# Half-height and half-width products held until their partner is ready, and the meta keys' product cut into such pairs

## The chip, the cores and the metric

The kernel runs on one core of a Trainium2 chip. The metric is the device time of one launch in microseconds, the median of several executions. TensorE (PE) multiplies, ScalarE (ACT) and VectorE (DVE) work on what it leaves in PSUM, GpSimd (POOL) does little, and SyncE (SP) issues most loads.

## What is computed

Three layers run in one launch over 512 positions of width 1024, in float32: a hybrid layer with a feed-forward part, then layer "ab" and layer "cd" over the 512 positions and 16 meta tokens ahead of them. The change touches four pieces of the last two layers:

```python
# layer ab, eight heads of 64: each query attends to its 128 best keys
logits = einsum('bqhd,bqkhd->bhqk', qb, kg) * dh ** -0.5 + bias
p = softmax(where(ok, logits, NEG_INF_2))
out = einsum('bhqk,bqkhd->bqhd', p, vg)
# layer ab, gated linear attention, and layer cd, retention: four heads of 64 (values 128)
att = where(causal, q @ k.T, 0)                  # retention: times a decay matrix
o = att @ v + (q * decay_in) @ S                 # S: state before the block
S = S * decay + (k * decay_out).T @ v
# layer cd, stick breaking: eight heads of 64
w = exp(log_sigmoid(z) + after)                  # z = q @ k.T, masked
out = einsum('bhqs,bshd->bqhd', w, v)
```

## The kernel before

Most of PE's work is the projections: `f_acc` (L164) multiplies a 128x128 block of weights with 256, 272 or 512 positions, three products for each block (high by high, high by low, low by high part in fp32r). While a projection runs, `tick` steps a generator of `self.bg` (L85), in which the attention and the linear layers stand as pipelines (`pipe`). So a few small products at a time stand between the projections' products. The order on each engine is then made by the framework's scheduler from the program's dependences and priorities (`first`, `chain`), and PE runs its list strictly in that order.

Four kinds of small product use a part of the 128x128 array. All four are plain float32, and each leaves two records in the trace:

- Values of the chosen keys (`dsa`, function `values`). For a pair of heads `f` and a block of 128 queries `i`, L1109 gives the 64 channels of head `e` = 0 in rows 0 to 63 of `o` and those of `e` = 1 in rows 64 to 127, for each block `j` of 128 keys. So a product has 128 rows of the array and 64 columns, and the two heads' use different columns. The 16 meta keys of both heads stand in one product at L1111 with 48 rows: rows 0 to 15 for one head, 32 to 47 for the other, and `avm` holds zeros elsewhere. Its right side comes from `em` (L1083), which `turn` transposes (L194) and copies out of PSUM (L1097).
- `linear`, scores (L1235) and state part (L1260): 64 channels of a head are rows 0 to 63 or 64 to 127, and heads with `e` = 0 and 1 use different rows and write different PSUM tiles. L1258 beside them uses the whole array, and L1213 (`update`) 64 columns.
- `stick`, values (L1354): 128 keys by 64 columns for each of two heads (`i` = 0, 1), for a block `b` of keys and 16 to 512 queries. Their right sides are the exponentials `wt` of L1342, one for each head.

For the two heads of one step the pipelines give the two products one after the other in the program, but nothing keeps them together in PE's order.

Of the kernel before, what the change touches and what calls it, by code (L numbers as in the profile page):

```python
# [8 lines left out]
F32 = mybir.dt.float32  # L9
# [3 lines left out]
AF = mybir.ActivationFunctionType  # L13
# [6 lines left out]
M = 16  # L20
# [40 lines left out]
class Kern:  # L61
# [56 lines left out]
    def behind(self, ins, name):  # L118

        if name and name != ins.name:  # L120
            self.tc.add_manual_dep(ins, name, mybir.DependencyInfo(mybir.DependencyClass.NoSync, mybir.DependencyReason.DATA), reason="order")

    def queue(self, q, out, src):

# [771 lines left out]
    def layer_ab(self, act, acc):  # L896
        nc, tc = self.nc, self.tc
# [3 lines left out]
        with tc.tile_pool(name="ab", bufs=1, reuse_waits="tile") as p:  # L901
# [30 lines left out]
            with self.chain():  # L932
                ps = self.ch("b")
# [61 lines left out]

            av = p.tile([128, 4, 512], F32, name="av")

            avm = p.tile([48, 4, 128], F32, name="avm")
            em = [p.tile([128, 48], F32, name=f"em{b}") for b in range(2)]
            for t in (avm, *em):  # L1000
                nc.gpsimd.memset(t, 0.0)

# [5 lines left out]
            av = av, avm, em  # L1008
# [41 lines left out]
    def dsa(self, p, cols, av, ag, masks, segs):  # L1050

        f, qs, ks = cols
        nc = self.nc
        av, avm, em = av
        bh = p.tile([128, 2, T], F32, name="bh", bufs=1)
        self.sheared(bh, self.tab2[2 * f:2 * f + 2], N2)
        tiles = {}
        held = []

        def logits(i, hh):  # L1060
# [24 lines left out]

        def turn(i, hh, n, q0, W, e, d):
            pT = p.tile([128, 5, 128], F32, name="pT", bufs=3)
            nb = i + 1
            if nb:
                pt = self.ch("b")  # L1090
                for j in range(nb):
                    self.transpose(pt[:, j * 128:(j + 1) * 128], e[:, M + j * 128:M + (j + 1) * 128])
                nc.scalar.copy(pT[:, :nb], pt[:, :nb * 128].rearrange("p (j q) -> p j q", j=nb))
            if hh == 1:
                pt = self.ch("b")
                self.transpose(pt[:48, :n], em[i % 2][:n])
                nc.vector.tensor_copy(pT[:48, 4, :n], pt[:48, :n])  # L1097
            return i, hh, n, q0, pT, d

        def values(i, hh, n, q0, pT, d):  # L1100
            held.append(pT)
            if hh == 0:
                return
            o = self.ch("o")[:, :n]

            for j in range(i + 1):
                for e in range(2):
                    c = (2 * f + e) * 64
                    nc.tensor.matmul(o[64 * e:64 * e + 64], lhsT=av[:, j, c:c + 64], rhs=held[e][:, j, :n], start=j == 0, stop=False,  # L1109
                                     skip_group_check=True)  # L1110
            nc.tensor.matmul(o, lhsT=avm[:, f], rhs=pT[:48, 4, :n], start=i < 0, stop=True, skip_group_check=True)  # L1111
            held.clear()
            rd = p.tile([128, 128], F32, name="rd", bufs=2)
            nc.vector.reciprocal(d[:n], d[:n])
            nc.scalar.copy(rd[:n].rearrange("p (h d) -> p h d", h=2), d[:n].to_broadcast([n, 2, 64]))
            return n, q0, o, rd

# [74 lines left out]
    def linear(self, p, q, k, kx, qs, ks, v, vm, decay, att, masked, out, meta, pace):  # L1192
# [3 lines left out]
        nc = self.nc  # L1196
# [28 lines left out]
        def scores(t, c0, n, vv):  # L1225
            if t == 0 and not meta:
                keys(-1, 0, M)
            if t < 3:
                keys(t, c0, n)
            a = att(t)  # L1230
            ps = self.ch("a"), self.ch("a")

            pairs = [(f, e, 64 * e) for f in range(2) for e in range(2)]
            for f, e, r0 in pairs:
                nc.tensor.matmul(ps[e][:n, f * n:f * n + n], lhsT=k[r0:r0 + 64, f, c0:c0 + n], rhs=q[r0:r0 + 64, f, c0:c0 + n], start=True, stop=True)  # L1235
            if kx is not None and n > 64:
                for f, e, r0 in pairs:
                    nc.tensor.matmul(ps[e][:64, f * n + 64:f * n + n], lhsT=kx[r0:r0 + 64, f, c0:c0 + 64], rhs=q[r0:r0 + 64, f, c0 + 64:c0 + n],
                                     start=True, stop=True)
            with self.chain():  # L1240
                for e in range(2):
                    masked(a[:n, e::2, :n], ps[e][:n, :2 * n].rearrange("p (h c) -> p h c", h=2), n, e)
            return t, c0, n, vv, a

        def attend(t, c0, n, vv, a):
            if t == 0 and not meta:
                update(-1, vm, M)
            st = state[0]
            osq = p.tile([128, T], F32, name="osq", tag="e", bufs=4 if meta else 2)[:, :512].rearrange("p (h c) -> p h c", h=4)
            rs = p.tile([128, 4], F32, name="rs", bufs=2)  # L1250
            om = self.ch("o"), self.ch("b")
            for inter in range(1 if st is None else 2):
                for f in range(2):
                    for e in range(2):
                        h, r0 = 2 * f + e, 64 * e
                        o = om[e][:n, f * 128:f * 128 + 128]
                        if not inter:
                            nc.tensor.matmul(o, lhsT=a[:n, h, :n], rhs=vv[:n, h * 128:h * 128 + 128], start=f == 0, stop=st is None, skip_group_check=True)  # L1258
                        else:
                            nc.tensor.matmul(o, lhsT=qs[r0:r0 + 64, f, c0:c0 + n], rhs=st[r0:r0 + 64, f], start=False, stop=True, skip_group_check=True)  # L1260
# [27 lines left out]
    def stick(self, p, cols, dv, od):  # L1288


        f, qs, ks = cols
        nc = self.nc
        om = []
        total = [None, None]
        held = []
# [29 lines left out]
        def sums(hh, b, n, c0, w, z, L, parts):  # L1325
# [16 lines left out]
            nc.scalar.activation(wt, z, AF.Exp)  # L1342
            return hh, b, n, c0, wt

        def values(hh, b, n, c0, wt):
            held.append(wt)
            if hh == 0:
                return
            if not om:
                om.append(self.ch("o"))  # L1350

            for i in range(2):
                h = 2 * f + i
                nc.tensor.matmul(om[0][64 * i:64 * i + 64, c0 - M:], lhsT=dv[:n, b, h * 64:h * 64 + 64], rhs=held.pop(0),  # L1354
                                 start=b == 4, stop=b == 0, skip_group_check=True)
            if b == 0:
                with self.chain():
                    nc.vector.tensor_tensor(out=od[:, f, M:], in0=om[0], in1=od[:, f, M:], op=OP.mult)
# [350 lines left out]
```

## Time and profile before

| | |
|---|---|
| Median of 3 runs | 1211.96 us (1211.02 to 1212.45) |
| The profiled execution | 1211.16 us |
| Its span, first to last instruction | 1209.4 us |
| PE busy, share of the span | 98% |
| DVE, ACT, POOL busy | 66%, 51%, 4% |
| Share of PE in the chain that ended last | 89% |
| Granted TensorE clock, mean | 0.995 |

The profiled execution took 1.8 us more than its span, and 0.8 us less than the median. Busy time of PE counts each product from its start to its modelled end, and products overlap in it, so what a product costs is read from the distance of starts.

### The profile page before, as it was taken

Reading aid. Unit: us, or ns where it says so; the run is one execution under the profiler, and the core shown is the slowest. Engines: PE = TensorE matmul, PEld = TensorE weight load, DVE = VectorE, ACT = ScalarE, POOL = GpSimd, SP = SyncE. Lnnn points to the kernel's source line nnn. Section 1 sums busy time; section 2 is a strip of 40 time slices with the busy share of each in tenths; the row PEclk is TensorE's granted clock in tenths of the full one; section 3 lists DMA queues with packets and bytes.
Section 4 is the critical chain, followed back from the end, with each engine's and each line's share of the span. In section 5 each row is a group of like instructions: output and inputs, shape, how many; then the busy total and the mean of one; then the engine's idle time right before and its main releaser. Section 6 shows DMA issues by size and latency. Waiting matters only on the chain.

```text
span 1209.4 us, 18772 instructions
## 1 busy us (share of the span) xinstructions
PE 1186.9 (98%) x7150; PEld 1014.7 (84%) x7150; DVE 800.5 (66%) x1810; ACT 618.7 (51%) x1377; POOL 51.4 (4%) x79
## 2 busy tenths in 40 slices
PE   8999899999999999999999999999999999999997
PEld 7988678888888888888999899888899889876776
DVE  6999966444434444455799999656575576775772
ACT  5588556333323333344454355666463575575753
POOL 7000002000000000011000000000020000000000
PEclk9999999999999999999999999999999999999999
DMA  7321122323233332234221122222132213220121
GB/s 253 110 78 60 46 71 88 103 89 105 72 98 113 102 97 95 85 96 123 89 71 61 46 71 71 70 71 71 54 111 84 87 53 106 70 70 18 53 87 70
DMA packets 32906, 101.81 MB, mean 84 GB/s; under 512 B 4128, under 2 KB 4960, under 8 KB 32816
## 3 DMA queue, kind: packets, MB, share of 16 engines
q1 hardware_dynamic: 30784, 96.48, 25.6%
q0 software_dynamic: 880, 2.25, 0.7%
q10 hardware_dynamic: 1152, 1.89, 0.5%
q8 instruction: 56, 0.92, 0.3%
q14 instruction: 34, 0.28, 0.1%
HBM read 96.42 MB, written 3.10 MB: 82 GB/s over the span
## 4 chain that ended last, share of the span: by engine, by line
PE 89%; DVE 6%; ACT 3%; DMA 1%; issue 1%; DVEq 0%; ACTq 0%
PE mm L164 68%; PE psb L194 4%; PE mm L183 2%; PE pso L1354 1%; DVE wlo L150 1%; PE pso L1109 1%; PE psa L1479 1%; PE mm L1479 1%; ACT whi L149 1%; PE pso L1111 1%; PE pso L642 1%; DVE sc L965 1%; PE psa L1328 1%; DMA x<-in_x 1%; PE psa L1073 1%
## 5 line engine op out<-in xcount | busy, mean ns | idle before, releaser
L164 PE MATMUL mm<-hhi,whi 128*128 128x512 f32 (+2 forms) x1280 | 433.5, 339 | 0.0
L164 PE MATMUL mm<-hlo,whi 128*128 128x512 f32 (+2 forms) x1280 | 426.6, 333 | 0.0
L164 PE MATMUL mm<-hhi,wlo 128*128 128x512 f32 (+2 forms) x1280 | 426.5, 333 | 0.0
L149 ACT CAST whi<-wraw 128x512 fp32r<-128x512 f32 x346 | 205.4, 594 | 314.2 <-PE mm L164 294.9
L150 DVE TENSOR_TENSOR wlo<-wraw,whi 128x512 fp32r<-128x512 f32 x346 | 231.5, 672 | 143.5 <-ACT whi L149 120.0
L164 PEld LDWEIGHTS mm<-hhi,whi 128*128 128x128 f32 x1280 | 242.4, 189 | 23.9 <-issue 2.0
L164 PEld LDWEIGHTS mm<-hhi,wlo 128*128 128x128 f32 x1280 | 241.9, 189 | 21.7 <-issue 0.3
L164 PEld LDWEIGHTS mm<-hlo,whi 128*128 128x128 f32 x1280 | 242.1, 189 | 21.0 <-issue 0.2
L164 PE MATMUL mm<-mx,whi 128*128 128x512 f32 (+2 forms) x448 | 112.8, 340 | 5.2 <-ACT mx L112 4.5
L164 PEld LDWEIGHTS mm<-mx,whi 128*128 128x128 f32 x448 | 76.2, 191 | 17.2 <-ACT mx L112 5.6
L786 DVE TENSOR_TENSOR gu<-mm,rb 128x512 f32<-128x512 f32 x44 | 30.4, 692 | 68.9 <-PE mm L164 66.8
L164 PE MATMUL mm<-mx,wlo 128*128 128x512 f32 (+2 forms) x224 | 74.8, 334 | 0.0
L164 PE MATMUL mm<-hidh,whi 128*128 128x512 f32 x176 | 68.5, 389 | 0.0
L164 PE MATMUL mm<-hidl,whi 128*128 128x512 f32 x176 | 68.5, 389 | 0.0
L164 PE MATMUL mm<-hidh,wlo 128*128 128x512 f32 x176 | 68.5, 389 | 0.0
L256 POOL TENSOR_TENSOR acc<-acc,sq 128x528 f32<-128x528 f32 (+1 forms) x18 | 25.7, 1428 | 778.1 <-ACT sq L254 461.0
L326 DVE TENSOR_TENSOR tmp<-mm,rb 128x272 f32<-128x272 f32 (+2 forms) x76 | 35.7, 469 | 27.4 <-PE mm L164 26.8
L164 PEld LDWEIGHTS mm<-mx,wlo 128*128 128x128 f32 x224 | 42.7, 190 | 3.5
L681 DVE SCALAR_TENSOR_TENSOR y<-u,cols,y 128x512 f32<-128x512 f32 x60 | 42.7, 745 | 1.2 <-ACT y L679 1.0
L314 DVE TENSOR_TENSOR x<-x,mm 128x512 f32<-128x512 f32 (+2 forms) x56 | 30.0, 536 | 15.5 <-PE mm L164 15.0
L164 PEld LDWEIGHTS mm<-hidh,whi 128*128 128x128 f32 x176 | 33.0, 188 | 6.9
L164 PEld LDWEIGHTS mm<-hidl,whi 128*128 128x128 f32 x176 | 33.0, 188 | 6.9
(434 smaller groups left out, 1794.9 us busy)
## 6 DMA issues: line engine op xcount, KB each, us to landing
wraw<-in_w SPq DMA_DIRECT2D x144, 512.0 KB, 3.5
wraw<-in_w SPq DMA_DIRECT2D x16, 384.0 KB, 3.0
wraw<-in_w SPq DMA_DIRECT2D x16, 320.0 KB, 2.8
bh<-tab SPq DMA_DIRECT2D x16, 132.0 KB, 2.9
mx<-cqk SPq DMA_DIRECT2D x8, 132.0 KB, 2.4
x<-in_x SPq DMA_DIRECT2D x4, 256.0 KB, 5.3
B<-tab POOLq DMA_DIRECT2D x4, 256.0 KB, 7.2
out<-L ACTq DMA_DIRECT2D x4, 256.0 KB, 2.5
```

Of the source, the lines that this page charges most:

```text
L149: self.nc.scalar.copy(hi[:, :w], raw[:, c])
L150: self.lo.tensor_tensor(out=lo[:, :w], in0=raw[:, c], in1=hi[:, :w].bitcast(F32), op=OP.subtract)
L164: nc.tensor.matmul(ps[b], lhsT=ww[i][:, f0:f0 + nf], rhs=aa[:, t0:t1], start=first and i == 0 and j == 0, stop=last and i == n - 1 and j == 2)
L183: nc.tensor.matmul(part(t), lhsT=aa[:, t0:t0 + nt], rhs=ww[i], start=u + i + j == 0 and t % 2 == 0, stop=u == 1 and i == 3 and j == 2, ski ...
L194: self.nc.tensor.transpose(out, in_, self.ident[:n, :n])
L256: e.tensor_tensor(out=acc[:, c0:c1], in0=acc[:, c0:c1], in1=sq[:, c0:c1], op=OP.add)
L314: nc.vector.tensor_tensor(out=x, in0=x, in1=p, op=OP.add)
L326: self.nc.vector.tensor_tensor(out=out[:, t0:t1], in0=p, in1=rb[:nf, t0:t1], op=OP.mult)
L642: nc.tensor.matmul(o[:, h * 64:h * 64 + 64], lhsT=pT[:, j * 128:(j + 1) * 128], rhs=vt[:, j, h * 64:h * 64 + 64], start=j == 0, stop=j == i)
L681: nc.vector.scalar_tensor_tensor(y[:, f], u[:, f, k:k + S], cw[:, f, k:k + 1], y[:, f], op0=OP.mult, op1=OP.add)
L786: nc.vector.tensor_tensor(out=t[:, g], in0=ps, in1=rbx, op=OP.mult)
L1479: nc.tensor.matmul(ps[half], lhsT=aa[:, c], rhs=ww[:, :512], start=False, stop=k == 3 and j == 2, skip_group_check=True)
```

## The change

`one_by_one` chains the products of the linear layers' scores and attention in the order of the program, in which the two halves of the array take turns. `ready` lets the first product of a pair wait for what the second needs as well: in `values` of `dsa` the first product of a block waits for the copies of head 1 (`made[1]`), in `stick` the first of two waits for the second's exponential. The meta keys' product becomes two, one for each head, with 128 rows and 64 columns, as the others of its block; for that `avm` and `em` grow to 128 rows or columns of which most are zero, and the copy at L1097 moves from DVE to ACT and from 48 rows to 128.

```diff
+    def one_by_one(self, inss):
+        for a, b in zip(inss, inss[1:]):
+            self.behind(b.ins, a.ins.name)
+
+    def ready(self, ins, names):
+        for name in names:
+            self.tc.add_manual_dep(ins, name, ...Sync...)
...
-            avm = p.tile([48, 4, 128], F32, name="avm")
-            em = [p.tile([128, 48], F32, name=f"em{b}") for b in range(2)]
+            avm = p.tile([128, 4, 128], F32, name="avm")
+            em = [p.tile([128, 128], F32, name=f"em{b}") for b in range(2)]
...
             if hh == 1:
                 pt = self.ch("b")
-                self.transpose(pt[:48, :n], em[i % 2][:n])
-                nc.vector.tensor_copy(pT[:48, 4, :n], pt[:48, :n])
+                self.transpose(pt[:, :n], em[i % 2][:n])
+                made[hh].append(nc.scalar.copy(pT[:, 4, :n], pt[:, :n]).ins.name)
...
-            for j in range(i + 1):
+            for j in [*range(i + 1), 4]:
                 for e in range(2):
                     c = (2 * f + e) * 64
-                    nc.tensor.matmul(o[64 * e:64 * e + 64], lhsT=av[:, j, c:c + 64], rhs=held[e][:, j, :n], start=j == 0, stop=False,
-                                     skip_group_check=True)
-            nc.tensor.matmul(o, lhsT=avm[:, f], rhs=pT[:48, 4, :n], start=i < 0, stop=True, skip_group_check=True)
+                    w, x = (avm[:, f, 64 * e:64 * e + 64], pT) if j == 4 else (av[:, j, c:c + 64], held[e])
+                    ins = nc.tensor.matmul(o[64 * e:64 * e + 64], lhsT=w, rhs=x[:, j, :n], start=i < 0 or j == 0, stop=j == 4,
+                                           skip_group_check=True)
+                    if j in (0, 4) and e == 0 and (i < 0 or j == 0):
+                        self.ready(ins.ins, made[1])
...
+            self.one_by_one(inss)      # linear: after the scores, and after the attention's products
...
-                nc.tensor.matmul(om[0][64 * i:64 * i + 64, c0 - M:], ...)   # stick
+                ins = nc.tensor.matmul(om[0][64 * i:64 * i + 64, c0 - M:], ...)
+                if i == 0:
+                    self.ready(ins.ins, [name])
```

The next rows are of PE's list before, second pair of heads (`f` = 1), first block of queries. L1109 is a head's product, L1111 the meta keys', L194 a transposition, L1073 to L1076 logits, L164 a projection.

```order
L1109 MATMUL pso<-pT,av 64x128
L164 MATMUL mm<-hhi,wlo 128x256
L194 MATMUL psb<-keep,em_6251 48x128
L1109 MATMUL pso<-pT,av 64x128
L1073 MATMUL psa<-qk 128x400
L1074 MATMUL psa<-qk 128x400
L1076 LDWEIGHTS identb
L1076 MATMUL psa<-mk_5945,identb 128x400
L194 MATMUL psb<-keep,e 128x128 x2
L1111 MATMUL pso<-pT,avm 128x128
```

The same block in the changed kernel, where the lines are some ten to twenty further down (L1122 for L1109 and L1111, L204 for L194, L1084 for L1073):

```order
L204 MATMUL psb<-keep,em_6251 128x128
L204 MATMUL psb<-keep,e 128x128 x2
L1084 MATMUL psa<-qk 128x272
L1085 MATMUL psa<-qk 128x272
L1122 MATMUL pso<-pT,av 64x128 x2
L1122 MATMUL pso<-pT,avm 64x128 x2
```

The two heads' products moved together and behind the transposition of `em`, and the meta keys' product became a pair right behind them.

In layer cd, third pair of heads of `stick` (L1354) beside the start of retention (L1213 state, L1235 scores), PE's list before reads:

```order
L1354 MATMUL pso<-wt,dv 64x512
L1328 MATMUL psb<-Lh,trir 128x512
L194 MATMUL psb<-keep,mx 128x128 x2
L1328 MATMUL psb<-Ll,trir 128x512
L1333 MATMUL psb<-Sh,mones 128x400
L1333 MATMUL psb<-Sl,mones 128x400
L1213 MATMUL psb<-cvm,kst 64x128 x4
L1235 MATMUL psa<-cqk 128x128
L1354 MATMUL pso<-wt,dv 64x512
```

The same two values now (L1373), with four scores (L1250) ahead of them:

```order
L1347 MATMUL psb<-Ll,trir 128x512
L1352 MATMUL psb<-Sh,mones 128x400
L1352 MATMUL psb<-Sl,mones 128x400
L1250 MATMUL psa<-cqk 128x128 x4
L1373 MATMUL pso<-wt,dv 64x512 x2
```

The first value moved behind all that stood between it and its partner.

A little later in that list, one block of retention's attention before (L1258 within the block, L1260 with the state):

```order
L1258 MATMUL psb<-cv,att 128x128 x2
L1260 MATMUL psb<-S,mx 128x128 x2
L1213 MATMUL psb<-cv,kst 64x128
L1258 MATMUL pso<-cv,att 128x128 x2
L1260 MATMUL pso<-S,mx 128x128 x2
L1213 MATMUL psb<-cv,kst 64x128 x3
L1235 MATMUL psa<-cqk 128x128 x3
```

And now (L1275, L1277, L1227 and L1250 are the same four lines):

```order
L1275 MATMUL pso<-cv,att 128x128
L1275 MATMUL psb<-cv,att 128x128
L1275 MATMUL pso<-cv,att 128x128
L1275 MATMUL psb<-cv,att 128x128
L1277 MATMUL pso<-S,mx 128x128
L1277 MATMUL psb<-S,mx 128x128
L1277 MATMUL pso<-S,mx 128x128
L1277 MATMUL psb<-S,mx 128x128
L1227 MATMUL psb<-cv,kst 64x128 x4
L1250 MATMUL psa<-cqk 128x128 x4
```

The two PSUM tiles, that is the two halves of the array's rows, take turns, and kinds no longer alternate.

## Rows read from the trace of the kernel before

**Rows 1.** The page: busy time, and the chain that ended last.

```profile
PE 1186.9 (98%) x7150; PEld 1014.7 (84%) x7150; DVE 800.5 (66%) x1810; ACT 618.7 (51%) x1377; POOL 51.4 (4%) x79
...
PE 89%; DVE 6%; ACT 3%; DMA 1%; issue 1%; DVEq 0%; ACTq 0%
```

**Rows 2.** Windows: stretch, length; PE, PEld, DVE, ACT, POOL busy; clock, DMA, GB/s.

```profile
645.00:700.00 55.00, 53.64 (x483) 48.83 (x482) 53.43 (x170) 19.19 (x48) 0.00 (x0) 1.00 0.21 65
710.00:880.00 170.00, 167.79 (x1325) 151.06 (x1325) 120.29 (x342) 99.70 (x261) 0.00 (x0) 0.99 0.22 66
945.00:1175.00 230.00, 229.27 (x1388) 182.23 (x1387) 156.31 (x329) 147.59 (x354) 0.00 (x0) 1.00 0.23 68
```

**Rows 3.** Waits of PE, 710 to 880: total us, times, longest.

```profile
PE psb L194 <- ACT em L1083: 1.0, 2, 0.7
...
PE pso L1111 <- DVE pT L1097: 0.4, 1, 0.4
```

**Rows 4.** Timeline of PE: start, length in us, instruction; values with meta keys.

```profile
834.19 0.88 PE L1109 MATMUL pso<-pT,av 128*64 128x128 f32 x12
834.99 0.49 PE L1111 MATMUL pso<-pT,avm 48*128 48x128 f32 x2
...
839.17 0.28 PE L164 MATMUL mm<-hhi,wlo 128*128 128x256 f32 x1
839.38 1.09 PE L1109 MATMUL pso<-pT,av 128*64 128x128 f32 x16
840.40 0.49 PE L1111 MATMUL pso<-pT,avm 48*128 48x128 f32 x2
...
841.16 0.29 PE L164 MATMUL mm<-hhi,wlo 128*128 128x256 f32 x1
```

**Rows 5.** Timeline of PE: two heads' products alone between projections.

```profile
744.93 0.44 PE L1109 MATMUL pso<-pT,av 128*64 128x128 f32 x4 [0.27 <-DVE ag L1123]
...
745.65 0.28 PE L164 MATMUL mm<-hhi,wlo 128*128 128x256 f32 x1
```

**Rows 6.** Timeline of PE: one head's product alone, then a transposition of `em`.

```profile
772.51 0.43 PE L1109 MATMUL pso<-pT,av 128*64 128x128 f32 x2
...
773.21 0.28 PE L164 MATMUL mm<-hlo,whi 128*128 128x256 f32 x1
773.33 0.27 PE L194 MATMUL psb<-keep,em 128*48 128x128 f32 x1
...
773.67 0.28 PE L164 MATMUL mm<-hlo,whi 128*128 128x256 f32 x1
```

**Rows 7.** Timeline of PE: stick's values of 512 queries, pair and single.

```profile
996.06 0.29 PE L164 MATMUL mm<-hhi,wlo 128*128 128x272 f32 x1
996.28 1.08 PE L1354 MATMUL pso<-wt,dv 128*64 128x512 f32 x4
...
997.64 0.29 PE L164 MATMUL mm<-hhi,wlo 128*128 128x272 f32 x1
...
1166.31 0.39 PE L164 MATMUL mm<-mx,whi 128*128 128x512 f32 x1
1166.63 1.07 PE L1354 MATMUL pso<-wt,dv 128*64 128x512 f32 x2
...
1168.20 0.62 PE L164 MATMUL mm<-mx,whi 128*128 128x512 f32 x2
```

**Rows 8.** Timeline of PE: the linear layer's state products, one half, then both.

```profile
684.92 0.71 PE L1260 MATMUL pso<-S,mx 64*128 64x128 f32 x4
685.56 0.71 PE L1258 MATMUL psb<-bv,att 128*128 128x128 f32 x4
...
694.36 0.37 PE L1260 MATMUL pso<-S,mx 64*128 64x128 f32 x1
...
695.00 0.38 PE L164 MATMUL mm<-hhi,whi 128*128 128x256 f32 x1
```

**Rows 9.** Line L1093, ACT's copies of transposed exponentials: count, duration in ns.

```profile
L1093 ACT COPY pT<-psb x32: 248/416/589, 726.9 to 871.0; 128x128 f32<-128x128 f32 x8, 128x256 f32<-128x256 f32 x8, 128x384 f32<-128x384 f32 x8, 128x512 f32<-128x512 f32 x8
```

More of the change, by code (lines that the diff above doesn't have):

```diff
@@ L121, in behind @@
             self.tc.add_manual_dep(ins, name, mybir.DependencyInfo(mybir.DependencyClass.NoSync, mybir.DependencyReason.DATA), reason="order")
+    def one_by_one(self, inss):
[3 more added lines that the diff above has]
+        for name in names:
+            self.tc.add_manual_dep(ins, name, mybir.DependencyInfo(mybir.DependencyClass.Sync, mybir.DependencyReason.DATA), reason="together")
     def queue(self, q, out, src):
@@ L1058, in dsa @@
         held = []
+        made = {}
         def logits(i, hh):
@@ L1087, in turn @@
             pT = p.tile([128, 5, 128], F32, name="pT", bufs=3)
+            made[hh] = []
             nb = i + 1
@@ L1092, in turn @@
                     self.transpose(pt[:, j * 128:(j + 1) * 128], e[:, M + j * 128:M + (j + 1) * 128])
-                nc.scalar.copy(pT[:, :nb], pt[:, :nb * 128].rearrange("p (j q) -> p j q", j=nb))
+                made[hh].append(nc.scalar.copy(pT[:, :nb], pt[:, :nb * 128].rearrange("p (j q) -> p j q", j=nb)).ins.name)
             if hh == 1:
                 pt = self.ch("b")
-                self.transpose(pt[:48, :n], em[i % 2][:n])
-                nc.vector.tensor_copy(pT[:48, 4, :n], pt[:48, :n])
+                self.transpose(pt[:, :n], em[i % 2][:n])
+                made[hh].append(nc.scalar.copy(pT[:, 4, :n], pt[:, :n]).ins.name)
             return i, hh, n, q0, pT, d
@@ L1233, in scores @@
             pairs = [(f, e, 64 * e) for f in range(2) for e in range(2)]
+            inss = []
             for f, e, r0 in pairs:
-                nc.tensor.matmul(ps[e][:n, f * n:f * n + n], lhsT=k[r0:r0 + 64, f, c0:c0 + n], rhs=q[r0:r0 + 64, f, c0:c0 + n], start=True, stop=True)
+                inss.append(nc.tensor.matmul(ps[e][:n, f * n:f * n + n], lhsT=k[r0:r0 + 64, f, c0:c0 + n], rhs=q[r0:r0 + 64, f, c0:c0 + n], start=True, stop=True))
             if kx is not None and n > 64:
                 for f, e, r0 in pairs:
-                    nc.tensor.matmul(ps[e][:64, f * n + 64:f * n + n], lhsT=kx[r0:r0 + 64, f, c0:c0 + 64], rhs=q[r0:r0 + 64, f, c0 + 64:c0 + n],
-                                     start=True, stop=True)
+                    inss.append(nc.tensor.matmul(ps[e][:64, f * n + 64:f * n + n], lhsT=kx[r0:r0 + 64, f, c0:c0 + 64], rhs=q[r0:r0 + 64, f, c0 + 64:c0 + n],
+                                                 start=True, stop=True))
+            self.one_by_one(inss)
             with self.chain():
@@ L1251, in attend @@
             om = self.ch("o"), self.ch("b")
+            inss = []
             for inter in range(1 if st is None else 2):
@@ L1257, in attend @@
                         if not inter:
-                            nc.tensor.matmul(o, lhsT=a[:n, h, :n], rhs=vv[:n, h * 128:h * 128 + 128], start=f == 0, stop=st is None, skip_group_check=True)
+                            ins = nc.tensor.matmul(o, lhsT=a[:n, h, :n], rhs=vv[:n, h * 128:h * 128 + 128], start=f == 0, stop=st is None, skip_group_check=True)
                         else:
-                            nc.tensor.matmul(o, lhsT=qs[r0:r0 + 64, f, c0:c0 + n], rhs=st[r0:r0 + 64, f], start=False, stop=True, skip_group_check=True)
+                            ins = nc.tensor.matmul(o, lhsT=qs[r0:r0 + 64, f, c0:c0 + n], rhs=st[r0:r0 + 64, f], start=False, stop=True, skip_group_check=True)
+                        inss.append(ins)
+            self.one_by_one(inss)
             oms = [o[:n, :256].rearrange("p (f d) -> p f d", f=2) for o in om]
@@ L1341, in sums, with values @@
             wt = p.tile([128, S], F32, name="wt", bufs=2)[:n, :w]
-            nc.scalar.activation(wt, z, AF.Exp)
-            return hh, b, n, c0, wt
-        def values(hh, b, n, c0, wt):
+            name = nc.scalar.activation(wt, z, AF.Exp).ins.name
+            return hh, b, n, c0, wt, name
+        def values(hh, b, n, c0, wt, name):
             held.append(wt)
@@ L1353, in values @@
                 h = 2 * f + i
-                nc.tensor.matmul(om[0][64 * i:64 * i + 64, c0 - M:], lhsT=dv[:n, b, h * 64:h * 64 + 64], rhs=held.pop(0),
+                ins = nc.tensor.matmul(om[0][64 * i:64 * i + 64, c0 - M:], lhsT=dv[:n, b, h * 64:h * 64 + 64], rhs=held.pop(0),
                                  start=b == 4, stop=b == 0, skip_group_check=True)
+                if i == 0:
+                    self.ready(ins.ins, [name])
             if b == 0:
```

## The prediction

> **What bounds the kernel now.** I read the page first: PE is busy for 98% of the span, and 89% of the chain that ended last is PE's own work [rows 1]. Then the windows of the stretches that the change touches: from 945 to 1175 us (layer cd) PE is busy for 229.27 of 230 us, from 710 to 880 (the chosen keys' attention) for 167.79 of 170 [rows 2]. There what PE does no longer comes off the end. Only from 645 to 700, where gated linear attention stands beside the choice of keys, is DVE as busy as PE (53.43 and 53.64 of 55). Then PE's waits in the chosen keys' attention: four groups of some 2.1 us together, of which the largest is 1.0, and one is the meta keys' product that waits 0.4 for its copy [rows 3]. So PE hardly waits, its list is executed in order, and the question is what each product costs in the list. That is read from the distance of starts in the timeline.
>
> **What the four kinds of product cost now.** A projection's product of 256 positions is 0.12 us from the next start (773.21 to 773.33, [rows 6]), one of 512 is 0.23 (a group of two is 0.62 long, a group of one 0.39, [rows 7]).
>
> - A pair of heads' products alone (four records): from 744.93 to 745.65, with two projections' products between, that is 0.72 - 0.24 = 0.48 us [rows 5]. Ahead of such a product the start comes 0.09 late (839.17 to 839.38 in place of 0.12, [rows 4]). Sum 0.57.
> - One head's product alone (two records): 772.51 to 773.21, also with two between: 0.70 - 0.24 + 0.09 = 0.55 [rows 6]. So a single costs what a pair costs: the two halves of the array run side by side.
> - Three pairs take 0.80 us up to the meta keys' product and four take 1.02 [rows 4]: 0.22 for each further pair, which I call a slot. The 0.57 of a pair alone is then a slot and 0.35 of something that is paid once for each visit, by which I mean a stretch of such products between products on the whole array.
> - The visit with four pairs and the meta keys: 839.17 to 841.16 less three projections' products is 1.63 us. Less 0.35 and four slots, the 48-row product costs 0.40: a slot and 0.18 for the change from one shape to the other.
> - Stick's values of 512 queries: the pair is 996.06 to 997.64 less three products of 0.12, 1.22 us. The single is 1166.31 to 1168.20 less three of 0.23, 1.20 [rows 7]. Again the same, and 0.85 of it is the slot. For fewer queries I scale the slot (estimates from this row): 0.66 for 400, 0.45 for 272, 0.24 for 144, 0.03 for 16.
> - The state products of the linear layer: two of one half take 0.64 us (684.92 to 685.56), four that alternate take 0.64 (694.36 to 695.00) [rows 8].
>
> The Trainium skill says in TensorEngine Tiling (Array Packing), Key Properties, that a change of the tiling mode drains TensorE. The 0.35 agrees with that, and the page gives no size. But the rows limit it: the transposition of `em`, 48 columns wide, stands between two projections' products and costs 773.21 to 773.67 less three times 0.12, 0.10 us, with nothing paid for the visit [rows 6].
>
> **The change part by part**, counted in PE's list before and after.
>
> *Chosen keys' values.* Before, the 16 blocks of 128 queries are 24 visits (the first two pairs of heads take 16, the last two 8), after it 16: 8 x 0.35 = 2.8 us. Five slots more than needed go to heads without their partner: 5 x 0.22 = 1.1. Of the 16 meta keys' products 12 stand behind pairs; each turns from 0.40 into a slot, 12 x 0.18 = 2.2. The other four stand alone and are among the 8 visits. The meta tokens' own four rows (16 queries) stay four visits; what they change is under 0.1 us each and left out. Sum 6.1 us less.
>
> *Stick's values.* Of 20 steps 12 are pairs already. The other eight are 16 singles, all in the last two pairs of heads: two steps of 512, two of 400, two of 272, one of 144, one of 16. Each step loses one visit with its slot: 2 x 1.20 + 2 x 1.01 + 2 x 0.80 + 0.59 + 0.38 = 7.0. Three of those singles share a visit with retention's products today and save 0.18 in place of 0.35: 0.5 off. Sum 6.5 us less.
>
> *Linear layers.* In retention 12 visits with 34 slots and six changes of shape become 10 with 26 and four: 0.70 + 1.76 + 0.36 = 2.8 us less. In gated linear attention the slots stay 40, and there is one visit more, since the chain lets the first score slip ahead alone in two blocks: 0.35 more. Sum 2.5 us less.
>
> *Transposition and copy of the meta keys.* The wider transposition costs PE what it cost: 0.10 us against 0.11 to 0.12 for one of 128 columns. 20 copies of 48 rows leave DVE and 20 of 128x128 come to ACT at about the 0.25 us of its narrowest copy [rows 9]. ACT is busy for 99.7 of 170 us there, so these 5 us lie beside PE's projections; if that cover were gone, they would be paid in part as the wait below. The memsets grow in their partitions alone, and POOL is idle.
>
> *The new waits.* PE is strict, so behind a first product that waits stands everything. Stick's singles move down to their partner, and the partner's exponential was waited for anyway; no cost. In the chosen keys' values the first product now needs the copy of the transposed `em` too, and nothing of the block can cover it. In 15 of the 20 visits PE has 0.8 us or more to do between that transposition and the visit. In five it has 0.22, 0.34, 0.47, 0.47 and 0.58 (their two to five instructions, at 0.11 to 0.13). The chain is at least 0.27 of transposition and 0.25 of copy, 0.52: short by 0.6 us in all. With a copy of head 1's exponentials (median 0.416) ahead of it on ACT the chain is 0.94, short by 2.6 in all. I take the middle, 1.5 us, since ACT is a little more than half busy.
>
> **Sum.** 6.1 + 6.5 + 2.5 - 1.5 = 13.6 us less. Against its own time of 1211.16 the profiled execution would come to 1197.6; the median of the runs lies 0.8 higher, so I forecast 1198.4 (0.989 of before).
>
> **The rivals.**
>
> 1. *The held products wait in earnest.* For it speaks that a wait at the head of a visit stops the whole of PE, and that the meta keys' product already waits 0.4 us in one place [rows 3]. If each of the 16 blocks waits that 0.4, that is 6.4 in place of 1.5: 1203.3. Against it: in the last two pairs of heads some twelve projections' products of 0.12 stand ahead of every visit. 15%.
> 2. *The rule of the drain holds for all shapes.* If 64 columns cost a visit whatever the instruction, the 16 transpositions of `em` for whole blocks, now on the whole array, would save 16 x 0.35 = 5.6 us more: 1192.8. [...] Against it stands the 0.10 us of [rows 6]. 5%.
> 3. *Nothing arrives at the end.* DVE is busy for 97% of 645 to 700 and 71% of 710 to 880 [rows 2]; if its list were the real limit, PE's gain would turn into waits for masks and evictions, and for layer cd, at 68% DVE, into waits for the sums. The time would stay at 1212. Against it: PE waits 2.1 us there now, and the nearly two thirds of the gain (9.3 of 15.1) that lie in layer cd meet an idle third of DVE. 5%.
> 4. *Slower.* ACT serves its list in order too. If each of the 16 blocks finds two 512-wide copies (0.589 us each, [rows 9]) ahead of the copy of `em` when PE stands at its first product, that is 16 x 1.18 = 18.9 us of wait against 15.1 gained: 1215.8. It decides from 0.94 us of wait a block on. Against it: in 15 of 20 visits PE arrives 0.8 us or more after the transposition. 4%.
>
> The forecast itself has 71%.
>
> **How the numbers follow.** The bounds of the wait (0 and 2.6) and an error of a tenth in the visits' price (1.5 us) give 1195 to 1201 for the likeliest case alone. The range reaches to the first rival and nearly to the second: 1193 to 1204. About 0.2% (2.4 us) is what a measurement of this kernel can tell from no change. Faster by more: forecast, rivals 1 and 2, 0.91. Within it: rival 3, 0.05. Slower: rival 4, 0.04.
>
> **What would show it.** In the changed trace the chosen keys' values should be 16 visits of pairs with the meta pair a further 0.22 us each, and no 48-row product. Stick's values should be 20 groups of four records, each as long as a single now (1.07 at 512). PE's waits from 710 to 880 should stay under some 4 us, with the copy on L1097's successor as their first cause. Wrong are the steps if a pair takes two slots; if visits without a wait cost clearly more or less than 0.35; or if PE's waits grow by more than 10 us, for then the gain was spent at the head of the held pairs.

## The result and the profile after

The kernel before took 1212.20 us in the median of the runs beside it (4, from 1211.02 to 1212.68), the changed one 1196.73 (4, from 1196.31 to 1198.57): a ratio of 0.9877, with an interval of 0.9860 to 0.9894. That is 15.5 us less; 13.6 were forecast, 1198.4 in place of 1196.73. The profiled execution took 1198.57, 12.6 less than the one of before.

The page of the changed kernel, its rows of busy time and of the chain that ended last:

```profile
PE 1174.6 (98%) x7190; PEld 1007.9 (84%) x7190; DVE 796.7 (67%) x1790; ACT 622.2 (52%) x1397; POOL 52.3 (4%) x79
...
PE 88%; DVE 6%; ACT 3%; DMA 1%; issue 1%; DVEq 0%; ACTq 0%
```

Beside [rows 1] PE has 40 instructions more (20 meta keys' products of two records each became pairs) and is busy 12.3 us less; ACT has the 20 copies that DVE gave up. PE's busy time fell by nearly what the span fell (12.6): the gain comes from products that stand closer together, and the change left the share that PE waits at 2%.

Windows of the changed kernel (stretch, length; PE, PEld, DVE, ACT and POOL busy; granted clock, DMA share, GB/s):

```profile
141.50:145.00 3.50, 2.94 (x6) 1.93 (x7) 3.50 (x7) 1.01 (x2) 0.00 (x0) 0.55 0.44 146
145.00:148.60 3.60, 3.60 (x10) 2.73 (x10) 2.42 (x5) 0.00 (x0) 0.00 (x0) 0.50 0.49 149
...
645.00:700.00 55.00, 53.73 (x482) 48.83 (x481) 53.05 (x167) 19.90 (x49) 0.00 (x0) 1.00 0.19 59
710.00:880.00 170.00, 168.00 (x1412) 154.41 (x1411) 122.02 (x338) 105.66 (x286) 0.00 (x0) 0.99 0.21 66
945.00:1165.00 220.00, 218.92 (x1380) 176.82 (x1379) 157.26 (x331) 148.14 (x354) 0.00 (x0) 1.00 0.23 70
...
720.00:725.00 5.00, 3.89 (x31) 3.29 (x29) 5.00 (x16) 3.00 (x14) 0.00 (x0) 1.00 0.36 107
725.00:729.00 4.00, 4.00 (x24) 3.85 (x23) 3.44 (x12) 2.87 (x6) 0.00 (x0) 0.57 0.01 4
...
1120.00:1126.40 6.40, 6.15 (x33) 4.64 (x31) 4.63 (x13) 4.39 (x15) 0.00 (x0) 1.00 0.28 76
1126.40:1133.20 6.80, 6.80 (x37) 5.29 (x37) 5.29 (x13) 6.28 (x19) 0.00 (x0) 1.00 0.08 15
```

In the chosen keys' attention (710 to 880) PE is busy for 168.00 of 170 us as it was for 167.79 [rows 2], but with 87 more instructions in the same stretch. From 945 on it idles 1.08 of 220 us against 0.73 of 230. ACT took 6 us more from 710 to 880, where it has 64 us to spare.

Where the 12.6 us lie, by the starts of the same projection's product in the two traces, after less before: +0.79 us at 200 us, before the first part of the change; a further +0.28 by the end of gated linear attention; -5.6 in the chosen keys' attention; -8.05 in layer cd, all of it after 1068 us, where the last two pairs of heads of `stick` and retention begin. The first 0.79 is no part of the change: it arises between 141 and 149 us, where PE's granted clock (1.00 is 2.4 GHz, 0.50 is 1.2 GHz) was lower in the changed kernel's execution. The first two windows above read, in the kernel before:

```profile
141.50:145.00 3.50, 2.32 (x6) 1.59 (x7) 3.50 (x7) 1.15 (x3) 0.00 (x0) 0.80 0.47 142
145.00:148.60 3.60, 3.60 (x13) 2.83 (x13) 3.11 (x6) 0.00 (x0) 0.00 (x0) 0.72 0.49 154
```

So the clock was 0.80 and 0.72 there, and 0.55 and 0.50 in the changed kernel. This one execution is also the longest of the changed kernel's four, so the medians (15.5 apart) are what the prediction is held against.

The waits of PE in the changed kernel, 705 to 870 us (total, times, longest):

```profile
PE psb L204 <- ACT em L1094: 1.0, 2, 0.7
PE psa L1084 <- DVE nm L1088: 0.7, 2, 0.4
```

The first row is that of [rows 3] unchanged. The wait for the copy of the transposed `em`, which the change made longer in principle, is not among them. The values themselves, line 1122 (duration in ns: shortest, median, longest; first and last start; forms):

```profile
L1122 PE MATMUL pso<-pT,av x160: 272/273/323, 738.1 to 868.8; 128*64 128x128 f32 x160
...
L1122 PE MATMUL pso<-pT,avm x80: 209/272/273, 724.8 to 869.0; 128*64 128x128 f32 x64, 128*64 128x16 f32 x16
```

All products of the values have 64 columns now, and they form 20 visits: 16 of blocks and four of meta tokens. PE idles ahead of none of these 240 records; before it idled 0.27 us ahead of a block's values [rows 5] and 0.4 ahead of a meta keys' product [rows 3]. Only the side that loads the weights (PEld) has idle times here, 0.9 us in five places, of 0.15 to 0.17 us each. By its modelled ends PE is still busy with earlier products then, and the other visits show nearly as much (0.08 to 0.15). By the distances of starts three visits begin late, by some 0.2 us in all. So no wait of the size of the forecast's 1.5 us is in this trace.

The timeline of PE in the changed kernel (start, length in us, instruction), a block with four pairs and the meta keys, then a pair of `stick` with 512 queries:

```profile
835.56 0.28 PE L174 MATMUL mm<-hhi,wlo 128*128 128x256 f32 x1
835.76 1.09 PE L1122 MATMUL pso<-pT,av 128*64 128x128 f32 x16
836.69 0.39 PE L1122 MATMUL pso<-pT,avm 128*64 128x128 f32 x4
837.01 0.39 PE L174 MATMUL mm<-hhi,whi 128*128 128x256 f32 x1
837.23 0.28 PE L174 MATMUL mm<-hlo,whi 128*128 128x256 f32 x1
...
1158.12 1.08 PE L1373 MATMUL pso<-wt,dv 128*64 128x512 f32 x4 [0.27 <-ACT wt L1361]
1159.12 0.50 PE L174 MATMUL mm<-mx,whi 128*128 128x512 f32 x1
1159.46 0.39 PE L174 MATMUL mm<-mx,wlo 128*128 128x512 f32 x1
```

The first visit takes 835.56 to 837.23 less two projections' products of 0.12, 1.43 us; with the price of the prediction it is 0.35 + 5 x 0.22 = 1.45, and before it was 1.63 [rows 4]. The pair of `stick` takes 1158.12 to 1159.46 less one product of 0.23, and with the 0.09 by which such a visit starts late 1.20 us: as long as a single was in [rows 7], for twice the work. `stick` has 20 such groups of four records now.

### The profile page after: what moved, and what is told of

It is laid out like the page before. It is cut to its first block, busy times and chain, and to the rows that moved or that the text cites. A ratio compares the mean times of both kernels' runs of the same rounds, so it can differ in the third digit from the quotient of the medians.

```text
span 1196.8 us, 18861 instructions
## 1 busy us (share of the span) xinstructions
PE 1174.6 (98%) x7190; PEld 1007.9 (84%) x7190; DVE 796.7 (67%) x1790; ACT 622.2 (52%) x1397; POOL 52.3 (4%) x79
## 4 chain that ended last, share of the span: by engine, by line
PE 88%; DVE 6%; ACT 3%; DMA 1%; issue 1%; DVEq 0%; ACTq 0%
PE mm L174 69%; PE psb L204 4%; PE mm L193 2%; PE pso L1122 1%; DVE wlo L160 1%; PE psa L1500 1%; PE mm L1500 1%; PE pso L1373 1%; ACT whi L159 1%; PE pso L652 1%; DMA x<-in_x 1%; PE psa L1347 1%; PE psa L1084 1%; PE psa L1085 0%; PE psa L956 0%
```

## The experiments

**The three parts apart.** What a version saves is read from its ratio to the runs of before beside it. The theory is that each visit of float32 products on a part of the array costs 0.35 us beside its slots. Each part was put into the kernel before alone. The linear layers' part:

```diff
...
+            self.one_by_one(inss)      # linear, both places; nothing else of the change
...
```

> Only the chain through the linear layers' products is added to the kernel before. Theory (visits and slots decide on a PE that never rests): by its own list the linear layers' visits change by some 1.7 us less at 0.35 a visit, 0.22 a slot and 0.18 a change of shape, so 1.5 to 2.8 us less, ratio 0.998 to 0.999. Rival (nothing arrives, another engine sets the pace): ratio 1.000. Rival (the lone first score of a block costs more than the pairing gives): slower by up to 1 us.

1209.22 us (11 runs), 0.9979 [0.9970, 0.9987] of before: 2.5 us less, with an interval of 1.6 to 3.6. The prediction's term was 2.5, the count of this kernel's own list 1.7: both are inside, and that the first is met to the tenth is chance.

`stick`'s part:

```diff
+            name = nc.scalar.activation(wt, z, AF.Exp).ins.name
...
+                if i == 0:
+                    self.ready(ins.ins, [name])
```

> Only stick's pair of values is held together. Theory: 16 singles become 8 pairs, seven visits less of their own and some joined ones, 6.3 to 6.5 us less, ratio 0.9947; PE's waits in layer cd stay under 1 us. Rival (nothing arrives): 1.000. Rival (held products wait): each of the 8 moved pairs waits 0.4 us, 3 us less, ratio 0.9974.

1206.28 us (5 runs), 0.9949 [0.9936, 0.9962]: 6.2 less, against 6.5.

The chosen keys' part, that is the changed kernel without the other two:

```diff
-            self.one_by_one(inss)
...
-                if i == 0:
-                    self.ready(ins.ins, [name])
```

> Only the chosen keys' part: held first products, and the meta keys' product as a pair. Theory: 6.1 us by visits, slots and shape changes, less 0.5 to 1.5 us of waits: 4.6 to 5.6 us less, ratio 0.9954 to 0.9962. Rival (held products wait in earnest): 16 x 0.4 us of waits eat the gain, ratio 0.999 to 1.000.

1207.77 us (6 runs), 0.9960 [0.9948, 0.9972]: 4.8 less, against 6.1 - 1.5 = 4.6. The three sum to 13.5 us, and their ratios multiply to 0.9888, inside the whole change's interval. So nothing shows that a part spoils another, and none carries the gain alone.

**The price by itself.** In the changed stretches a price could also be a wait that the trace does not name. So 44 groups of products on constants, whose results nobody reads, were put into the kernel before, behind projections of the feed-forward layer, where nothing is waited for. Eleven kinds take turns:

```diff
+        if kind == 0:
+            cols(m)            # two products of 64 columns, float32: a pair
+        elif kind == 1:
+            mm(o[:64, :128], lhsT=m[:, :64], rhs=m, **how)      # one of the two alone
+        elif kind == 2:
+            cols(m)
+            cols(m)
+        elif kind == 3:
+            mm(o[:, :128], lhsT=m, rhs=m, **how)                # whole array
+        elif kind == 4:
+            mm(o[:64, :128], lhsT=r[:, :64], rhs=r, **how)      # 64 columns in float32r
...
+            self.nc.tensor.transpose(o[:48, :128], m[:, :48], self.ident)
```

> The kernel before with 44 groups of products on constants between the feed-forward projections (one per projection, eleven kinds in turn, 128 columns of moving data, results not read). Theory: a group costs 0.35 us for the visit plus 0.22 for each float32 slot when it uses part of the array: pair by columns 0.57, one alone 0.57, two pairs 0.79, 64-row pair 0.57, 48 rows 0.57; a whole-array float32 product 0.22, a whole-array fp32r product 0.11, and a 48-column transposition 0.10. The one-pass shapes with 64 columns (fp32r alone, bf16 pair) are the open ones: 0.11 if only two-pass float32 pays for the visit, 0.46 if every shape does. Span up by 17 us in the first case, 19 to 21 us in the second. Rival (the 0.35 was a wait for another engine in the attention and not the array's): every group costs its slots alone, pairs 0.22, span up by some 8 us.

1229.94 us (one execution), 17.5 more than the 1212.49 of before beside it. The timeline of PE in this kernel, for each kind the product ahead, the group, and the fifth product behind it:

```profile
205.17 0.40 PE L164 MATMUL mm<-hhi,wlo 128*128 128x512 f32 x1
205.50 0.44 PE L778 MATMUL pso<-m 128*64 128x128 f32 x4
...
206.90 0.39 PE L164 MATMUL mm<-hlo,whi 128*128 128x512 f32 x1
...
211.22 0.39 PE L164 MATMUL mm<-hhi,wlo 128*128 128x512 f32 x1
211.54 0.43 PE L783 MATMUL pso<-m 128*64 128x128 f32 x2
...
212.94 0.39 PE L164 MATMUL mm<-hlo,whi 128*128 128x512 f32 x1
...
217.25 0.39 PE L164 MATMUL mm<-hhi,wlo 128*128 128x512 f32 x1
217.57 0.66 PE L778 MATMUL pso<-m 128*64 128x128 f32 x8
...
219.21 0.40 PE L164 MATMUL mm<-hlo,whi 128*128 128x512 f32 x1
...
258.47 0.40 PE L164 MATMUL mm<-hhi,wlo 128*128 128x512 f32 x1
258.70 0.27 PE L800 MATMUL pso<-keep,m 128*48 128x128 f32 x1
...
259.73 0.39 PE L164 MATMUL mm<-hlo,whi 128*128 128x512 f32 x1
```

Five projections' products of 0.227 us (1.135) taken off, a pair costs 0.59, a single 0.58 and two pairs 0.82 (from the starts to the nanosecond 0.586, 0.580 and 0.820; the four places of a kind agree within 0.01). The prediction's 0.57, 0.55 and 0.79 come from places inside the changed code. The further pair is 0.23, the visit 0.35. On the whole array a float32 product costs 0.25, one visit less. The transposition 48 columns wide costs 0.13 and float32r of 64 columns 0.15, against 0.13 for float32r on the whole array: they pay no visit. Float32 products of 64 rows, in pairs (0.64), and of 48 rows (0.63) pay it; so do a pair of 64 columns in bf16 (0.39) and a pair of 64 rows in float32r (0.47). PE idles ahead of none of these groups.

So the price is no wait for another engine, and a smaller number of columns alone does not make it. The loads of the weights (PEld) show where it lies. Two pairs, and the transposition:

```profile
217.57 0.42 PEld L778 LDWEIGHTS pso<-m 128*64 128x64 f32 x8 [0.35 <-PE mm L164]
...
218.16 0.19 PEld L164 LDWEIGHTS mm<-hhi,whi 128*128 128x128 f32 x1 [0.17 <-ACT whi L149]
218.16 0.50 PE L164 MATMUL mm<-hhi,whi 128*128 128x512 f32 x1
...
258.47 0.10 PEld L800 LDWEIGHTS pso<-keep,m 128*48 128x48 f32 x1
```

At both edges of the visit the load starts with its product (217.57 and 218.16) and not ahead of it; for the transposition it starts 0.23 us ahead (258.47, the product at 258.70). All seven kinds that pay show this at both edges, within 2 ns, and none of the other four does. The Trainium skill says in TensorEngine Tiling (Array Packing), Key Properties, that a change of the tiling mode drains TensorE. That agrees with the visits that pay (0.35 us in a place without waits); which operands change the mode that section does not say, and here a transposition of 48 columns (0.13) and float32r of 64 columns (0.15) did not pay. Why those two do not is not shown.

**What in the chosen keys' attention gains.** First the meta keys' pair without the hold, in the kernel of the third experiment:

```diff
-                    if j in (0, 4) and e == 0 and (i < 0 or j == 0):
-                        self.ready(ins.ins, made[1])
```

> The chosen keys' part alone, with the meta keys' product as a pair but without the hold: first products go as soon as their own head is ready. Theory: by its list 24 visits with 63 slots in place of 28 with 64, and no 48-row product: 3.8 us less than before, ratio 0.9969. Rival (the gain of the chosen keys' part is the hold alone): 1.000. Rival (the hold costs in waits what it gives): as with the hold or better, 0.996 or less.

1208.43 us (10 runs), 0.9971 [0.9962, 0.9980]: 3.5 less than before, against 3.8.

Then the hold with the 48-row product and its copy on DVE; here the first product waits for head 1's exponentials alone:

```diff
...
-            for j in [*range(i + 1), 4]:
+            for j in range(i + 1):
...
-                    if j in (0, 4) and e == 0 and (i < 0 or j == 0):
-                        self.ready(ins.ins, made[1])
+                    if j == e == 0:
+                        self.ready(ins.ins, made[1][:1])
...
+            nc.tensor.matmul(o, lhsT=avm[:, f], rhs=pT[:48, 4, :n], start=i < 0, stop=True, skip_group_check=True)
```

> The chosen keys' part alone, with first products held for the other head's copy but the meta keys' product left at 48 rows and its copy on VectorE. Theory: 22 visits with 60 slots in place of 28 with 64, the 48-row product kept: 2.6 us less than before less some 0.5 of waits, ratio 0.9978 to 0.9983. Rival (the gain is the pair of the meta keys alone): 1.000.

1209.63 us (11 runs), 0.9983 [0.9974, 0.9992]: 2.1 less, as expected. Both halves gain. Together they make 5.6 where the whole part made 4.8; each has an interval of about 1 us to both sides, so the sum does not show that one takes from the other.

**What the new wait costs.** The changed kernel with the meta keys' copy back on DVE, so that it stands behind no copy of ACT:

```diff
-                made[hh].append(nc.scalar.copy(pT[:, 4, :n], pt[:, :n]).ins.name)
+                made[hh].append(nc.vector.tensor_copy(pT[:, 4, :n], pt[:, :n]).ins.name)
```

> The changed kernel with one edit: the copy of the transposed meta keys' exponentials goes back to VectorE (128 rows). PE's list is the same but for what the scheduler moves. Theory (the new waits are small, 0.5 to 1.5 us in all, most of it a copy behind another copy on ScalarE): between 1 us less and 0.5 us more than the changed kernel, ratio to before 0.987 to 0.988. Rival (held products wait in earnest for ScalarE's queue): 3 us or more less than the changed kernel, ratio 0.985 or less.

1197.98 us (4 runs), 0.9884 [0.9868, 0.9899]: 1.25 us more than the changed kernel where 0.5 more was the most expected, but the intervals overlap nearly whole. Rival 1 (a wait of 6.4 us behind ACT) should have given 3 us or more back here. It did not. In the two traces, from 732 us to the end of the chosen keys' attention, this version is 0.8 us the shorter; PE idles ahead of none of the values here either.

**More shapes.** Eleven other kinds in the place of the first eleven, among them:

```diff
+            mm(o[:64, :128], lhsT=i[:, :64], rhs=i, **how)            # bf16, 64 columns, alone
+            cols(m)                                                   # columns, then rows
+            rows(m)
+            mm(o[:32, :128], lhsT=r[:32, :32], rhs=r[:32], **how)     # float32r, 32 x 32
...
+            mm(o[:64, :128], lhsT=m[:, :64], rhs=m, **how)            # single, whole array, single
+            mm(o[:, :128], lhsT=m, rhs=m, **how)
+            mm(o[64:128, :128], lhsT=m[:, :64], rhs=m, **how)
...
+            mm(o[64 * e:64 * e + 64, :128], lhsT=m[:, :64], rhs=m, **how)   # the same half twice
```

> As the price kernel, with eleven other groups. Theory (0.35 for a visit, 0.22 for each float32 slot of 128, 0.18 for a change of shape inside): column pair then 64-row pair 0.97, column pair then 48 rows 0.97, column single, whole-array product, column single 1.36, two row pairs 0.79, column pair of 16 moving columns 0.4, two products of the same half 0.79, whole-array bf16 0.12. Open: one bf16 product of 64 columns in either half, 0.39 if a part of the array is what costs, 0.12 if the turn between the halves is; fp32r on 32x32, 0.12, and on 16 rows by 128 columns, 0.46. Rival (the price hangs on the number of products and not on visits): group 6 costs what two products of the same half and a whole one cost, 1.04.

1240.85 us (one execution), 28.7 more than the 1212.20 of before beside it. The timeline of PE in this kernel, at float32r of 32 x 32, then at a column single, a product on the whole array and the other column single:

```profile
229.52 0.39 PE L164 MATMUL mm<-hhi,wlo 128*128 128x512 f32 x1
229.84 0.24 PE L791 MATMUL pso<-mones 32*32 32x128 f32 x1
230.01 0.50 PE L164 MATMUL mm<-hhi,whi 128*128 128x512 f32 x1
...
231.05 0.40 PE L164 MATMUL mm<-hlo,whi 128*128 128x512 f32 x1
...
241.28 0.39 PE L164 MATMUL mm<-hhi,wlo 128*128 128x512 f32 x1
241.60 0.43 PE L795 MATMUL pso<-m 128*64 128x128 f32 x2
241.96 0.49 PE L796 MATMUL pso<-m 128*128 128x128 f32 x2
242.38 0.43 PE L797 MATMUL pso<-m 128*64 128x128 f32 x2
...
243.77 0.39 PE L164 MATMUL mm<-hlo,whi 128*128 128x512 f32 x1
```

The second group tests the word visit. It costs 1.36 us, as was expected of two visits with a whole product between them, and not the 1.04 of the rival, by which the price hangs on the number of products. The first group costs 0.39, visit included, where float32r of 64 columns on all rows cost 0.15. A bf16 single costs 0.40, as its pair did. A pair of columns and then a pair of rows cost 1.01, 0.19 beyond a pair of columns and a further slot: a change between two shapes of parts is paid too, at about the 0.18 of the prediction. Two products of the same half take 0.81, no shorter than four of both halves (0.82). That puts the column halves side by side in a place without waits. In all ten kinds here that pay, the loads at both edges start with their products again.

**Fewer visits still.** If the price is right, joining more visits gains more. Four versions of the changed kernel, with further buffers for what is held: `stick`'s values of 16, 144 and 272 queries held for one visit and those of 400 and 512 for another; and the meta tokens' own rows, held for the visit of the first block.

```diff
-            if hh == 0:
+            if hh == 0 or b in (4, 3, 1):             # or (f < 2 and b in (4, 3, 1))
                 return
...
+            if i < 0:                                 # the meta tokens' own rows
+                if hh:
+                    low.append((n, q0, pT, d))
+                return
...
+            while low:                                # behind the first block's pairs
```

Both joins, for all four pairs of heads:

> The changed kernel with visits joined and no product taken away: stick holds the values of its steps of 16, 144 and 272 queries for one visit and those of 400 and 512 for another, and the chosen keys' values of the meta tokens' rows join the visit of the first block. Theory (each visit costs 0.35 whatever it holds): by its list 17 visits less, some with a change of shape in their place, 4.6 us less than the changed kernel, ratio to before 0.984. Rival (a visit costs only because the products around it are waited for): no gain, 0.9877. Rival (longer holding makes PE wait for exponentials or the end wait for the last visit): 0.99 or more.

1197.36 us (4 runs), 0.9887 [0.9872, 0.9902]: no gain where 4.6 us were expected; the theory missed. Windows of this kernel (columns as above):

```profile
1120.00:1126.40 6.40, 5.44 (x27) 3.87 (x26) 5.19 (x12) 6.40 (x23) 0.00 (x0) 1.00 0.21 68
1126.40:1133.20 6.80, 6.80 (x23) 5.21 (x22) 4.41 (x12) 4.39 (x13) 0.00 (x0) 0.50 0.03 13
```

In layer cd PE idles for 0.96 of 6.40 us, and then runs for 6.8 us at a granted clock of 0.50 (1.2 GHz) and gets 23 products done in place of 37. That costs half of 6.8, 3.4 us; the changed kernel idles for 0.25 there and keeps 1.00. The next three were meant to tell whether that stretch is the reason. The meta tokens' rows alone:

> The changed kernel with one edit: the values of the meta tokens' rows join the visit of the first block, four visits less. Theory (0.35 a visit): 1.4 us less than the changed kernel, ratio to before 0.9865. Rival (a visit that joins another saves nothing): 0.9877.

1198.36 us (5 runs), 0.9885 [0.9867, 0.9904]: another miss by the times: 1.4 us less than the changed kernel were expected, the median is 1.6 above it, and the two are not to be told apart. `stick`'s joins alone, all four pairs of heads:

> The changed kernel with stick's values joined alone: steps of 16, 144 and 272 queries in one visit, 400 and 512 in another, for all four pairs of heads. By visits 3.2 us less than the changed kernel, ratio to before 0.985. Theory on the miss of the version with all joins (a stretch of some 7 us near 1126 at the lower clock, behind short idle times of PE, takes 3.4 us): that stretch is there again and the ratio is 0.987 to 0.989. Rival (the loss lies in the meta tokens' join): no such stretch, 0.985.

1195.59 us (4 runs), 0.9863 [0.9842, 0.9884]: 1.1 less than the changed kernel, where 3.2 were the price of the visits. The stretch at 0.50 was expected here again, and did not come:

```profile
1120.00:1126.40 6.40, 5.96 (x32) 4.36 (x31) 4.55 (x11) 5.74 (x21) 0.00 (x0) 1.00 0.19 66
1126.40:1133.20 6.80, 6.17 (x31) 4.75 (x31) 6.44 (x17) 6.52 (x19) 0.00 (x0) 1.00 0.21 72
```

Both joins, but `stick`'s only in the first two pairs of heads, where projections stand between its steps:

> The changed kernel with the meta tokens' rows joined, and stick's values joined for the first two pairs of heads only, where projections stand between. By visits 3.1 us less than the changed kernel, ratio to before 0.985, and no stretch at the lower clock near 1126. Rival (a joined visit saves nothing): 0.9877.

1193.86 us (4 runs), 0.9851 [0.9834, 0.9869], with the clock at 1.00 in the stretch in question. It is the best version, 2.9 us below the changed kernel's median, against 3.1 expected; but the intervals overlap from 0.9860 to 0.9869.

The traces settle more than the times, by the starts of the same projection's product. The meta tokens' join shortens the chosen keys' attention by 1.2 us from 732 us on, in each of the three versions that have it (1.4 expected): the price holds, and what the traced execution with this join alone lost lies before 706 us, ahead of the join. `stick`'s joins in the first two pairs of heads give 1.7 us in each of the three versions that have them (1.7 expected). In the last two pairs they give 0.4 us without the stretch at 0.50 (1.5 expected), and lose 1.8 with it. There PE idles more for the longer holding: 1.7 us from 1060 us on in place of 0.8 in the changed kernel, in the version that keeps its clock. So the first version's miss has two parts in its trace: waits that the joins of the last two pairs bring, and the stretch at 0.50. Of the executions that were only timed the mean granted clock is known: 0.992, 0.992 and 0.993 in the first version, 0.996 to 0.997 in the changed kernel. Whether their loss stands at the same place stays open.

## Why the prediction was right

- **The kernel is bound by PE's list.** Shown: what was taken out of the list came off the end, part by part (2.5, 6.2 and 4.8 us for terms of 2.5, 6.5 and 4.6, each known to about 1 us). Rival 3 (the gain turns into waits for DVE) falls: PE is busy for 98% of the span after too, and DVE for 67% in place of 66%.
- **A visit costs 0.35 us, a further pair 0.22, and a single what a pair costs.** Shown three times: in the changed stretches (1.43 us for the five pairs against 1.45; 1.20 for `stick`'s pair of 512), in a place without any wait (0.35 and 0.23), and in the two singles with a whole product between them (1.36). The joined visits agree where PE did not wait (1.2 us for 1.4, 1.7 for 1.7).
- **The transposition pays nothing.** Shown: 0.13 us by itself. Rival 2, which would have given 5.6 us more, falls.
- **The new waits** were put at 1.5 us, between 0 and 2.6. The trace has them at the lower bound: PE idles ahead of none of the held values, and from 735 to 900 us it idles 0.9 us in all where it idled 1.1 before. The prediction took the middle of its bounds for want of better; the term was too high by nearly all of its size. It also named the copy of `em` as the first cause of what waits remain; the trace names `em` itself (L1094, 1.0 us), as before. Rivals 1 and 4 needed 6.4 and 18.9 us.
- **Sizes that were off, and luck.** In the two traces the chosen keys' attention gives 5.6 us for 4.6 (6.1 without the waits that did not come); gated linear attention costs 0.28 for 0.35; layer cd gives 8.05 where the terms are 6.5 + 2.8 = 9.3. The first error and the last cancel: that the changed stretches sum to 13.4 us in the traces for a forecast of 13.6 is in part luck, and the medians are 1.9 us off. Of layer cd's 1.25 us, 0.35 is idle time of PE that was not there before (1.08 against 0.73 us, in a stretch 10 us shorter), among it a pair of `stick` that waits 0.27 for its exponential, a wait that the prediction set at nothing. By the distances of starts `stick`'s own line gives 5.4 us and retention's four lines 2.7, which is the whole gain of this layer. The products at the edges of the visits, where each visit should cost some 0.2 (0.09 ahead, 0.11 behind), give nothing in sum, though the trace counts 19 visits in place of 27 from 1068 us on. Beyond the idle time that is not explained.
- **A small misreading.** The memsets were said to grow in partitions alone; `em` grew from 48 to 128 columns as well. POOL, busy for 52.3 us in place of 51.4, is not what bounds the kernel.

## What to carry to other kernels

On an engine that is busy for 98% of the span, count its list in visits and slots, not in instructions: a product on a part of the array paid 0.35 us here for standing alone between products on the whole of it, its partner on the other half came free, and a further pair cost 0.22. Find the price of a shape in a place where nothing waits before reordering for it: narrow operands did not all pay it (float32r of 64 columns and a transposition cost as little as on the whole array). Holding the first product for its partner cost little here while other work on the engine covered the partner's last copy, and it is worth a look at each place whether it does: the same joins gave 1.7 us where projections stood between, and 0.4 where PE had to wait longer for them.

## What was not expected of the hardware

PE's granted clock fell to its lower level (0.50, 1.2 GHz) after short idle times, and not in each execution of the same list. The changed kernel has a mean of 0.57 from 725 to 729 us, and 24 products in it. The version with `stick`'s joins alone executes the same products in the same order up to 900 us, and its windows read:

```profile
720.00:725.00 5.00, 3.89 (x31) 3.26 (x30) 5.00 (x18) 2.85 (x13) 0.00 (x0) 1.00 0.38 107
725.00:729.00 4.00, 4.00 (x32) 3.75 (x30) 3.78 (x11) 3.31 (x8) 0.00 (x0) 1.00 0.20 31
```

In both PE idles for 1.11 of the 5 us before 725, in two gaps of 0.4 and 0.7, and in one the clock then falls, in the other it stays at 1.00, with 32 products; the second execution gains 1.4 us on the first here. Such stretches come and go: before 730 us the profile of the version with the meta tokens' rows alone has four of them, that of the version with the copy on DVE one. And the time of an execution goes with its mean granted clock: in the four executions of the version with the copy on DVE 1194.98 us at 0.998, 1197.30 at 0.996, 1198.66 at 0.995 and 1199.10 at 0.994. So two single executions of one kernel can differ by 4 us with no change in the code behind it. A gain of that size is read from medians and intervals, or from the starts within one stretch of two traces, and not from two spans.
